# DeltaNet's convolution: the prompt's running sum moves into a PSUM bank, the key and recurrence chains get two banks instead of three, and sample rows get their own tanh

## The chip, the cores and the metric

The kernel runs on one core of a Trainium2 chip, in one launch. The metric is device time in microseconds. Names used below: TensorE (PE in the rows, PEld its weight loads) multiplies, VectorE (DVE), ScalarE (ACT) and GpSimd (POOL) work on tiles, SyncE (SP) issues DMAs. Each engine takes its instructions in the order in which they stand in its queue. PSUM is used here as eight banks of 128 x 512 fp32.

## The reference, cut to what matters

One step of a two-layer decoder: a gated DeltaNet layer with its feed-forward part, then a sparse-attention layer with its own. It is run for 512 prompt tokens and for 8 sample sequences of 4 tokens. The change touches the short convolution of the DeltaNet layer, and through the PSUM banks its key chain and recurrence:

```
def causal_short_conv(x, buf, w):
    xp = jnp.concatenate([buf.astype(x.dtype), x], axis=1)
    y = xp[:, 0:t] * w[0]
    for i in range(1, DN_CONV):              # DN_CONV = 4 taps
        y = y + xp[:, i:i + t] * w[i]
    return jax.nn.silu(y), xp[:, xp.shape[1] - (DN_CONV - 1):]
...
def step(S, xc):                             # recurrence over chunks
    U = wv_n - jnp.einsum('bhik,bhkv->bhiv', wk_n, S)
    O = jnp.einsum('bhik,bhkv->bhiv', qg_n, S) + jnp.einsum('bhij,bhjv->bhiv', aqk_n, U)
    S = gl_n[..., None, None] * S + jnp.einsum('bhik,bhiv->bhkv', kdec_n, U)
    return S, O
```

The convolved channels are q, k and v: 8 heads of 128 channels each, so 24 channel blocks. The silu is computed as a tanh and a product.

## The kernel before, in words

Channels lie on the 128 partitions, tokens along the free dimension: 512 prompt columns and 32 sample columns (8 x 4), 544 in all. A product with a weight is a `gemm` that takes both sides as a high and a low half and so issues three matmuls for each of 8 slices of the inner dimension (L177, L178, L179). A channel block is done in two halves of 256 and 288 columns, 24 matmuls each. `load_w` brings the weight in, casts the high half on ScalarE (L158) and subtracts for the low half on VectorE, or on GpSimd for q, v and z (L159).

`qkv(ty, h, ...)` makes one channel block; ty is 0 for q, 1 for k, 2 for v. ScalarE copies the gemm's banks into `pre` (L456, L458) and scales the first tap (L464). VectorE adds the other taps (L470); for q the second tap is made by ScalarE (L467) and added by GpSimd (L468). GpSimd makes the sample rows' sum with a product and an add for each tap (L475, L477). One tanh on ScalarE covers all 544 columns (L478); VectorE makes the prompt output (L479) and the sample output (L480).

`keys(h)`, K0 to K7 in the plan, turns a head's k block chunk by chunk: a transposition on TensorE (L525), a square with a sum on ScalarE (L526), products of k with itself (L533), which VectorE scales into BB (L535). After every fourth head DMAs put BB's diagonal blocks in DRAM. `diag_inverse(g)`, D0 and D1, takes four heads' blocks from there and solves them row by row on VectorE: a product L595 and a subtraction L597 for each step, 46 of each. ScalarE transposes the result (L600), DMAs carry it to DRAM and back, and `inverse(h)`, I0 to I7, builds the whole inverse of a chunk from it with small products (L621, L628, L629, L638, L641). `head(h)` is the recurrence over four chunks, whose products L722 to L729 depend on one another.

The plan of the DeltaNet part is a text: DN_START, then four pairs of heads whose recurrences are woven with other work, then a tail. In DN_START the letters k, q, v, z are channel blocks, the capitals what follows from them:

```
DN_START = "k0 K0 q1 k2 k1 K2 v1 k3 K1 z0 K3 S0 k4 q0 K4 Q0 v0 V1 D0 k5 q3 s0 v4 z1 Q1 V0 K5 s3 k6 k7 I0 q2 v3 I1 K6 Q3 K7 s2 Y0 Q2 s1 v2 V3"
```

The text sets the order in which the source is written. A scheduler then sorts each engine's queue by a simulated timeline, in which a tile has to be free before it is written; so the number of buffers of a tile decides what stands where. The banks are `mm` for gemms, `aux` for side products, and `ch` for the key chain and the recurrence.

Of the kernel before, what the change touches and what calls it, by code (L numbers as in the profile page):

```python
# [10 lines left out]
F32 = mybir.dt.float32  # L11
# [3 lines left out]
AF = mybir.ActivationFunctionType  # L15
OP = mybir.AluOpType
# [3 lines left out]
SEQ = 512  # L20
NB = 8
TS = 4
NS = NB * TS
NT = SEQ + NS
# [87 lines left out]
class Net:  # L112
# [206 lines left out]
    def deltanet(self, up, ctx):  # L319
        nc, A, O, T, V, S, G = self.nc, self.A, self.O, self.T, self.V, self.S, self.G  # L320
# [36 lines left out]
        wk = ctx.enter_context(tc.tile_pool(name="dnw", bufs=2))  # L357
# [16 lines left out]
        def decays():  # L374

            wab = self.load_w(W, 0, KD, 4 * D, 16)
            abf = wk.tile([128, NT], F32, name="cy")[0:16]
            for c0, cn in HALVES:
                ps = self.mm()[0:16, :cn]
                self.gemm(ps, wab, u, c0, cn)  # L380
# [26 lines left out]
            for n in (13, 11, 9, 7, 5, 3):  # L407
# [5 lines left out]
                                   op0=OP.mult, op1=OP.mult)  # L413
# [25 lines left out]
        def hb():  # L439

            return wk.tile([128, SEQ], F32, name="hb", tag="hb", bufs=HB)

        def qkv(ty, h, to, outS):

            o = to[h] = hb()
            ch = ty * 8 + h
            w = self.load_w(W, 0, KD, ch * 128, 128, pool_lo=ty != 1)
            pre = wk.tile([128, 515 + 56], F32, name="pre")
            pres = pre[:, 515:571].rearrange("p (b n) -> p b n", n=7)
            G.memset(pre[:, 0:3], 0.0)  # L450
            G.tensor_copy(pres[:, :, 0:3], hist[:, ch].rearrange("p (b n) -> p b n", n=3))
            for c0, cn in HALVES:
                ps = self.mm()[:, :cn]
                self.gemm(ps, w, u, c0, cn)
                n = min(cn, SEQ - c0)
                S.copy(pre[:, 3 + c0:3 + c0 + n], ps[:, 0:n])  # L456
                if n < cn:
                    S.copy(pres[:, :, 3:7], ps[:, n:cn].rearrange("p (b t) -> p b t", t=4))  # L458
                yield

            cw = [self.cw[:, i * 24 + ch:i * 24 + ch + 1] for i in range(4)]
            y = wk.tile([128, NT], F32, name="cy")
            th = wk.tile([128, NT], F32, name="cth", bufs=1)
            S.activation(y[:, 0:SEQ], pre[:, 0:SEQ], AF.Copy, scale=cw[0])  # L464
            if ty == 0:
                y2 = wk.tile([128, NT], F32, name="cth", bufs=1)[:, 0:SEQ]
                S.activation(y2, pre[:, 1:1 + SEQ], AF.Copy, scale=cw[1])  # L467
                G.tensor_tensor(y[:, 0:SEQ], y[:, 0:SEQ], y2, op=OP.add)  # L468
            for i in range(1 if ty else 2, 4):
                V.scalar_tensor_tensor(y[:, 0:SEQ], pre[:, i:i + SEQ], cw[i], y[:, 0:SEQ], op0=OP.mult, op1=OP.add)  # L470
            ys = y[:, SEQ:NT].rearrange("p (b t) -> p b t", t=4)
            ts = sm.tile([128, NB, TS], F32, name="cts")
            for i in range(4):
                wb = cw[i][:, :, None].to_broadcast([128, NB, TS])
                G.tensor_tensor(ts if i else ys, pres[:, :, i:i + 4], wb, op=OP.mult)  # L475
                if i:
                    G.tensor_tensor(ys, ys, ts, op=OP.add)  # L477
            S.activation(th, y, AF.Tanh)  # L478
            V.scalar_tensor_tensor(o, th[:, 0:SEQ], 1.0, y[:, 0:SEQ], op0=OP.add, op1=OP.mult)  # L479
            V.scalar_tensor_tensor(outS[:, h], th[:, SEQ:NT], 1.0, y[:, SEQ:NT], op0=OP.add, op1=OP.mult)  # L480

            g = h // 4
            left = rows.setdefault((ty, g), [sm.tile([128, 27, 4], F32, name=f"cl{ty}{g}", bufs=1), {*range(4 * g, 4 * g + 4)}])
            r = left[0]
            left[1].remove(h)
            S.copy(r[:, :, h % 4].rearrange("p (a b) -> p a b", b=3),
                   bass.AP(tensor=pre.tensor, offset=pre.offset + 512, ap=[list(pre.ap[0]), [7, 9], [1, 3]]))
            if not left[1]:
                pc = self.bank("ch")
                T.transpose(pc[0:108, 0:128], r.rearrange("p r h -> p (r h)"), ident)  # L490
                cso = wk.tile([108, 128], F32, name="cso", bufs=1)
                S.copy(cso, pc[0:108, 0:128])
                for dst, a, n in ((O["p_dn_conv"], 0, 3), (O["s_dn_conv"], 12, 24)):
                    self.dma(bass.AP(tensor=dst.tensor, offset=dst.offset + (8 * ty + 4 * g) * 128, ap=[[QKV, n], [128, 4], [1, 128]]),
                             cso[a:a + 4 * n])

        def kF(h):
            return qkv(1, h, kT, kS)
# [379 lines left out]
        def plan(text):  # L878
            return chain.from_iterable(make[t[0]](int(t[1])) for t in text.split())

        decays()
        run(plan(DN_START))
        for p, (text, inv, steps) in enumerate(DN_PAIRS):
# [860 lines left out]
    def run(self, ctx):  # L1744
# [4 lines left out]
        self.G.memset(self.nhalf, -0.5)  # L1749
        self.nvh = self.cst.tile([128, 1], F32, name="nvh")  # L1750
        self.cw = self.cst.tile([128, 96], F32, name="cw")
        self.banks(mm=3, aux=2, ch=3)
        with ExitStack() as c:
            og = self.deltanet(up, c)
        self.banks(mm=4, aux=4)
# [14 lines left out]
        with tc.tile_pool(name="nsa", bufs=1) as np_:  # L1770
# [6 lines left out]
            o = self.attention(ux, rstd, tiles, up, np_)  # L1777
# [39 lines left out]
```

## Time and profile before

| | |
|---|---|
| three runs, us | 1664.23, 1658.86, 1659.84; median 1659.84 |
| the profiled execution, us | 1663.51 |
| its span from first to last instruction, us | 1661.7 |
| mean granted TensorE clock | 0.985 |
| busy: TensorE, VectorE, ScalarE, GpSimd | 96%, 64%, 43%, 34% |
| DeltaNet part | from the start to about 400 us |

The rows below are of the profiled execution. A timeline row gives the start and the duration of an instruction (or of several of one form, x and their count), the engine, the source line, output and inputs; in brackets stands how long the engine was idle before it, and what ended that. Line numbers are those of the kernel before. Those of the changed kernel are one lower from L480 on (L525 is L524 there); within the convolution, scale, taps, tanh and output of the prompt are L466, L468, L469 and L470, the sample rows' products and adds L474 and L476, their tanh and output L478 and L479.

### The profile page before, as it was taken

How to read it: one execution, taken by the hardware profiler on the slowest of the kernel's cores; microseconds unless marked ns; L12 is line 12 of the kernel's file. 1: busy time of each engine (PE TensorE's matmuls, PEld its weight loads, DVE VectorE, ACT ScalarE, POOL GpSimd, SP SyncE). 2: the span in 40 equal slices, each digit the busy share in tenths (PEclk: the TensorE clock that was granted, in tenths of full speed). 3: DMA queues.
4: the chain of work that ended last, by engine and by line, in shares of the span. 5: the costliest groups of instructions: out<-in, count | busy, mean ns of one | idle time of the engine just before them, and what ended most of it. 6: DMA issues, size and time to landing. Idle time of an engine off the chain costs nothing.

```text
span 1661.7 us, 32748 instructions
## 1 busy us (share of the span) xinstructions
PE 1598.3 (96%) x12527; PEld 1528.5 (92%) x12527; DVE 1062.2 (64%) x2543; ACT 709.8 (43%) x1796; POOL 564.5 (34%) x861
## 2 busy tenths in 40 slices
PE   8998898998989999999999999999999999999997
PEld 7998788987989999999999999877999999999997
DVE  5879779487577753555556688678875553355533
ACT  5554554553323222232332487778843232132233
POOL 3675546424366711100145476565520000000000
PEclk9999999999999999999999999999999999999999
DMA  6233412257556634354342532523133332334222
GB/s 195 77 78 93 109 36 70 72 163 219 138 143 142 160 101 117 95 164 132 108 140 81 147 95 78 177 70 112 45 96 102 102 106 79 108 90 127 77 88 81
DMA packets 289069, 183.37 MB, mean 110 GB/s; under 512 B 25183, under 2 KB 271784, under 8 KB 288784
## 3 DMA queue, kind: packets, MB, share of 16 engines
q1 hardware_dynamic: 286352, 172.88, 37.5%
q0 software_dynamic: 2560, 8.39, 1.4%
q8 instruction: 99, 1.62, 0.4%
q14 instruction: 58, 0.48, 0.1%
HBM read 159.33 MB, written 26.90 MB: 112 GB/s over the span
## 4 chain that ended last, share of the span: by engine, by line
PE 77%; DVE 10%; POOL 4%; DMA 3%; ACT 3%; issue 2%; SPq 0%; POOLq 0%; DVEq 0%; ACTq 0%
PE mm L179 15%; PE mm L177 15%; PE mm L178 15%; PE aux L177 5%; PE aux L178 5%; PE aux L179 5%; PE po L1641 2%; PE aux L1668 2%; DVE hb L595 2%; DVE hb L597 1%; DVE wlo L159 1%; PE mm L1578 1%; PE mm L1579 1%; PE mm L818 1%; DVE cy L470 1%
## 5 line engine op out<-in xcount | busy, mean ns | idle before, releaser
L177 PE MATMUL mm<-uh,whi 128*128 128x288 f32 (+2 forms) x1824 | 531.3, 293 | 5.1 <-DVE hb L689 1.7
L179 PE MATMUL mm<-uh,wlo 128*128 128x288 f32 (+2 forms) x1824 | 523.8, 292 | 6.7 <-DVE wlo L159 6.7
L178 PE MATMUL mm<-ul,whi 128*128 128x288 f32 (+2 forms) x1824 | 530.1, 292 | 0.0
L158 ACT CAST whi<-wraw 128x1024 fp32r<-128x1024 f32 (+5 forms) x231 | 215.9, 936 | 524.0 <-PE mm L178 431.0
L177 PEld LDWEIGHTS mm<-uh,whi 128*128 128x128 f32 (+1 forms) x1824 | 343.9, 189 | 8.4 <-DVE hb L689 2.1
L179 PEld LDWEIGHTS mm<-uh,wlo 128*128 128x128 f32 (+1 forms) x1824 | 341.0, 189 | 9.2 <-DVE wlo L159 8.3
L178 PEld LDWEIGHTS mm<-ul,whi 128*128 128x128 f32 (+1 forms) x1824 | 344.3, 189 | 1.5 <-issue 0.4
L159 DVE TENSOR_TENSOR wlo<-wraw,whi 128x1024 fp32r<-128x1024 f32 (+5 forms) x207 | 235.5, 1138 | 118.6 <-ACT whi L158 117.2
L179 PE MATMUL aux<-uh,wlo 128*128 128x288 f32 (+1 forms) x704 | 202.7, 288 | 3.1 <-DVE wlo L159 3.1
L177 PE MATMUL aux<-uh,whi 128*128 128x288 f32 (+1 forms) x704 | 203.3, 289 | 0.0
L178 PE MATMUL aux<-ul,whi 128*128 128x288 f32 (+1 forms) x704 | 203.3, 289 | 0.0
L177 PE MATMUL mm<-hh,whi 128*128 128x256 f32 (+1 forms) x704 | 202.0, 289 | 0.0
L178 PE MATMUL mm<-hl,whi 128*128 128x256 f32 (+1 forms) x704 | 201.4, 288 | 0.0
L179 PE MATMUL mm<-hh,wlo 128*128 128x256 f32 (+1 forms) x704 | 196.5, 288 | 0.0
L179 PEld LDWEIGHTS aux<-uh,wlo 128*128 128x128 f32 x704 | 133.1, 189 | 3.6 <-DVE wlo L159 3.6
L184 POOL TENSOR_TENSOR ycol<-yvar,nhalf 128x2 f32<-128x2 f32 (+1 forms) x2 | 1.6, 775 | 390.2 <-DVE yvar L1716 390.2
L178 PEld LDWEIGHTS aux<-ul,whi 128*128 128x128 f32 x704 | 133.1, 189 | 0.0
L177 PEld LDWEIGHTS aux<-uh,whi 128*128 128x128 f32 x704 | 132.8, 189 | 0.2 <-issue 0.2
L178 PEld LDWEIGHTS mm<-hl,whi 128*128 128x128 f32 x704 | 132.6, 188 | 0.0
L177 PEld LDWEIGHTS mm<-hh,whi 128*128 128x128 f32 x704 | 132.6, 188 | 0.0
L179 PEld LDWEIGHTS mm<-hh,wlo 128*128 128x128 f32 x704 | 129.6, 188 | 0.0
L969 DVE SCALAR_TENSOR_TENSOR fup<-aux,rstd 128x256 f32<-128x256 f32 x88 | 38.6, 439 | 122.9 <-PE aux L179 122.9
(535 smaller groups left out, 2969.1 us busy)
## 6 DMA issues: line engine op xcount, KB each, us to landing
wraw<-in_ffn_w_in_dram SPq DMA_DIRECT2D x88, 512.0 KB
wraw<-in_dn_w_in_dram SPq DMA_DIRECT2D x32, 512.0 KB
wraw<-in_ffn_w_out_dram SPq DMA_DIRECT2D x32, 384.0 KB
wraw<-in_ffn_w_out_dram SPq DMA_DIRECT2D x32, 320.0 KB
hb<-in_state_dn_S_dram SPq DMA_DIRECT2D x32, 256.0 KB
wraw<-in_nsa_w_kv_dram SPq DMA_DIRECT2D x12, 512.0 KB
bskew<-bscr SPq DMA_DIRECT2D x16, 320.0 KB
x<-xd SPq DMA_DIRECT2D x16, 272.0 KB
```

Source lines behind the costliest of these rows:

```text
L158: self.S.copy(hi, src)
L159: (self.G if pool_lo else self.V).tensor_tensor(lo, src, hi.bitcast(F32), op=OP.subtract)
L177: self.T.matmul(ps, lhsT=hi[:, k, :], rhs=uh[:, cs], start=first and k == 0, stop=False)
L178: self.T.matmul(ps, lhsT=hi[:, k, :], rhs=ul[:, cs], start=False, stop=False)
L179: self.T.matmul(ps, lhsT=lo[:, k, :], rhs=uh[:, cs], start=False, stop=last and k == kc - 1)
L470: V.scalar_tensor_tensor(y[:, 0:SEQ], pre[:, i:i + SEQ], cw[i], y[:, 0:SEQ], op0=OP.mult, op1=OP.add)
L595: V.tensor_tensor(t, D[a][:, 0:m, l:l + 1].to_broadcast([64, m, n]), row.to_broadcast([64, m, n]), op=OP.mult)
L597: V.tensor_tensor(N[a][:, 0:m, l:32], N[a][:, 0:m, l:32], t, op=OP.subtract)
L818: T.matmul(ps, lhsT=Kh, rhs=um[q], start=True, stop=True)
L969: V.scalar_tensor_tensor(up, pu, 0.5, rstd[:, cs], op0=OP.mult, op1=OP.mult)
L1641: T.matmul(self.po, lhsT=self.VT[ty][:, kb, g], rhs=m[:, i:i + 2].rearrange("p e q -> p (e q)"), start=False, stop=last and kb > k0 and m ...
L1668: T.transpose(ps[:, i * 128:(i + 1) * 128], P[2 * pr + e][ty][:, a:a + 128], ident)
```

## The change

The running sum `y` of the prompt columns is no longer an SBUF tile with two buffers but a PSUM bank of its own with one buffer. The eight banks, split 3, 2 and 3 before, are split 3 (`mm`), 2 (`aux`), 2 (`ch`) and 1 (`cy`). For q too, all three later taps are made by VectorE. The sample rows keep an SBUF tile `ys`, and have their own tanh over 32 columns; the prompt's tanh over 512 columns and its output stand in the source ahead of the sample rows' sum.

```
-            abf = wk.tile([128, NT], F32, name="cy")[0:16]
+            abf = wk.tile([128, NT], F32, name="cth", bufs=1)[0:16]
...
-            y = wk.tile([128, NT], F32, name="cy")
+
+            y = self.bank("cy")
+            ys = wk.tile([128, NB, TS], F32, name="cy")
             th = wk.tile([128, NT], F32, name="cth", bufs=1)
-            S.activation(y[:, 0:SEQ], pre[:, 0:SEQ], AF.Copy, scale=cw[0])
-            if ty == 0:
-                y2 = wk.tile([128, NT], F32, name="cth", bufs=1)[:, 0:SEQ]
-                S.activation(y2, pre[:, 1:1 + SEQ], AF.Copy, scale=cw[1])
-                G.tensor_tensor(y[:, 0:SEQ], y[:, 0:SEQ], y2, op=OP.add)
-            for i in range(1 if ty else 2, 4):
-                V.scalar_tensor_tensor(y[:, 0:SEQ], pre[:, i:i + SEQ], cw[i], y[:, 0:SEQ], op0=OP.mult, op1=OP.add)
-            ys = y[:, SEQ:NT].rearrange("p (b t) -> p b t", t=4)
+            S.activation(y, pre[:, 0:SEQ], AF.Copy, scale=cw[0])
+            for i in range(1, 4):
+                V.scalar_tensor_tensor(y, pre[:, i:i + SEQ], cw[i], y, op0=OP.mult, op1=OP.add)
+            S.activation(th[:, 0:SEQ], y, AF.Tanh)
+            V.scalar_tensor_tensor(o, th[:, 0:SEQ], 1.0, y, op0=OP.add, op1=OP.mult)
             ts = sm.tile([128, NB, TS], F32, name="cts")
             for i in range(4):
                 wb = cw[i][:, :, None].to_broadcast([128, NB, TS])
                 G.tensor_tensor(ts if i else ys, pres[:, :, i:i + 4], wb, op=OP.mult)
                 if i:
                     G.tensor_tensor(ys, ys, ts, op=OP.add)
-            S.activation(th, y, AF.Tanh)
-            V.scalar_tensor_tensor(o, th[:, 0:SEQ], 1.0, y[:, 0:SEQ], op0=OP.add, op1=OP.mult)
-            V.scalar_tensor_tensor(outS[:, h], th[:, SEQ:NT], 1.0, y[:, SEQ:NT], op0=OP.add, op1=OP.mult)
+            ysf = ys.rearrange("p b t -> p (b t)")
+            S.activation(th[:, SEQ:NT], ysf, AF.Tanh)
+            V.scalar_tensor_tensor(outS[:, h], th[:, SEQ:NT], 1.0, ysf, op0=OP.add, op1=OP.mult)
...
-        self.banks(mm=3, aux=2, ch=3)
+        self.banks(mm=3, aux=2, ch=2, cy=1)
```

The scheduler's order moves with it. In the excerpts an x and a number after a shape count instructions, and the brackets name the engines and DMA queues whose semaphores an instruction waits for.

First, TensorE's queue at head 4's keys. Before, sample keys (L559, L562), the transpositions L525 and the products L533 stand among gemm matmuls:

```order
L559 MATMUL ch<-Bs,BsT 128x128 [waits DVE_49]
L525 MATMUL ch<-ct,hb 128x128 [waits Activation_49]
L705 MATMUL aux<-ct,hb 128x128 x2
L179 MATMUL mm<-uh,wlo 128x256
L533 MATMUL ch<-hb 128x128 [waits DVE_49,PE_49]
L533 MATMUL ch<-hb 128x128 x3
L177 MATMUL mm<-uh,whi 128x256
```

Of the change:

```order
L179 MATMUL mm<-uh,wlo 128x256
L524 MATMUL ch<-ct,hb 128x128 [waits DVE_49,PE_49]
L524 MATMUL ch<-ct,hb 128x128 [waits Activation_49]
L561 MATMUL ch<-B_1257,BsT 128x128 [waits DVE_49]
L524 MATMUL ch<-ct,hb 128x128 [waits Activation_49] x2
L532 MATMUL ch<-hb 128x128 [waits Activation_49]
L532 MATMUL ch<-hb 128x128 x3
L704 MATMUL aux<-ct,hb 128x128 [waits DVE_49]
L704 MATMUL aux<-ct,hb 128x128 x3
L515 MATMUL ch<-ct,Gc 128x128 [waits DVE_49]
L515 MATMUL ch<-ct,Gc 128x128 x3
L177 MATMUL mm<-uh,whi 128x288 [waits Activation_49]
```

The four transpositions of this head now follow one another with no gemm matmul between. The first of these products stood behind 588 gemm matmuls of DeltaNet and now stands behind 696; for head 3, whose products DMAs carry to D0, it is 475 and 539.

Second, ScalarE's queue where D0 ends (L600, and L599 in the change). Before:

```order
L458 COPY pre<-mm 128x8x4
L600 COPY hb<-hb 64x16x16 [waits DVE_49]
L600 COPY hb<-hb 64x16x16
L526 ACTIVATE junk_112,ssk<-ch 128x128 [waits PE_49]
L478 ACTIVATE cth<-cy 128x544 [waits DVE_49,Activation_49,Pool_49]
```

Of the change:

```order
L466 ACTIVATE cy<-pre,cw 128x512 [waits DVE_49,Pool_49]
L478 ACTIVATE cth<-cy 128x32 [waits Activation_49,Pool_49]
L485 COPY cl_1013<-pre 128x27 [waits Activation_49]
L525 ACTIVATE junk_112,ssk<-ch 128x128 [waits PE_49]
L469 ACTIVATE cth<-cy 128x512 [waits DVE_49]
L525 ACTIVATE junk_112,ssk<-ch 128x128 [waits PE_49]
L158 CAST whi<-wraw 128x1024 [waits DMAHW2_49,PE_49]
L646 ACTIVATE cth<-hb 128x512 [waits DVE_49]
L466 ACTIVATE cy<-pre,cw 128x512
L599 COPY hb<-hb 64x16x16 [waits DVE_49]
L599 COPY hb<-hb 64x16x16
```

The scale L466 of a block waits for VectorE, which has to be done with the block ahead in the one bank. The tanh of the sample rows stands ahead of that of the prompt. D0's copies come behind a cast that comes behind the start part's last gemms.

Third, TensorE's queue at the first inverse, I0. Before, its first products L621 stand among gemm matmuls, behind 978 of the 1008 that the start part has:

```order
L179 MATMUL mm<-uh,wlo 128x256
L621 MATMUL aux<-XT,BB 128x96 [waits DMAHW5_49,DMAHW4_49,DMAHW3_49]
L621 MATMUL aux<-XT,BB 128x96 x3
L177 MATMUL mm<-uh,whi 128x256
```

Of the change:

```order
L524 MATMUL ch<-ct,hb 128x128 [waits Activation_49]
L673 MATMUL ch<-ct,q2s 128x1 [waits Activation_49,Pool_49]
L620 MATMUL aux<-XT,BB 128x96 [waits DMAHW7_49,DMAHW6_49,DMAHW0_49]
L620 MATMUL aux<-XT,BB 128x96 x3
L675 MATMUL ch<-qS,kS 128x128 [waits DVE_49]
...
L637 MATMUL aux<-XT,BB 64x64 [waits DVE_49]
L637 MATMUL aux<-XT,BB 64x64 x3
L620 MATMUL aux<-XT,BB 128x96 [waits DVE_49,PE_49,Activation_49]
L620 MATMUL aux<-XT,BB 128x96 x3
L640 MATMUL aux<-XX,Y_120 64x64 [waits DMAHW5_49,DMAHW1_49,DVE_49]
```

All 1008 gemm matmuls of the start part now stand ahead of the first inverse, and none between the first (I0) and the second (I1), whose first products are the second L620.

## Rows read from the trace of the kernel before

**Rows 1.** The page's busy times (us, share of the span, instructions) and its chain by engine.

```profile
PE 1598.3 (96%) x12527; PEld 1528.5 (92%) x12527; DVE 1062.2 (64%) x2543; ACT 709.8 (43%) x1796; POOL 564.5 (34%) x861
...
PE 77%; DVE 10%; POOL 4%; DMA 3%; ACT 3%; issue 2%; SPq 0%; POOLq 0%; DVEq 0%; ACTq 0%
```

**Rows 2.** Busy time by stretch: length, each engine (instructions), clock, DMA share, GB/s.

```profile
118.50:179.20 60.70, 51.22 (x400) 48.45 (x399) 55.61 (x147) 27.31 (x71) 37.28 (x60) 0.94 0.30 80
179.20:200.00 20.80, 18.75 (x158) 17.96 (x158) 13.64 (x34) 13.08 (x42) 13.09 (x26) 0.92 0.63 147
200.00:212.00 12.00, 11.97 (x104) 9.16 (x105) 8.47 (x31) 6.89 (x22) 1.34 (x6) 1.00 0.38 84
```

**Rows 3.** TensorE's waits from 40 to 200: us in total, times, longest.

```profile
PE ch L525 <- ACT junk L526: 9.5, 3, 4.6
```

**Rows 4.** Timeline from 133 to 143: start, duration, engine, line, idle time before it.

```profile
135.56 4.17 POOL L477 TENSOR_TENSOR cy<-cy,cts 128x32 f32<-128x32 f32 x1
...
137.56 0.28 PE L179 MATMUL mm<-uh,wlo 128*128 128x256 f32 x1
...
140.78 0.25 POOL L477 TENSOR_TENSOR cy<-cy,cts 128x32 f32<-128x32 f32 x1
...
141.06 0.66 ACT L478 ACTIVATE cth<-cy 128x544 f32<-128x544 f32 x1 [6.38 <-POOL cy L477]
...
141.75 0.69 DVE L479 SCALAR_TENSOR_TENSOR hb<-cth,cy 128x512 f32<-128x512 f32 x1 [2.14 <-ACT cth L478]
...
142.44 0.48 PE L525 MATMUL ch<-ct,hb 128*128 128x128 f32 x1 [4.61 <-ACT junk L526]
```

**Rows 5.** Convolution lines, whole span: min/median/max ns and starts, or busy, mean | idle.

```profile
L470 DVE SCALAR_TENSOR_TENSOR cy<-pre,cw,cy x64: 645/750/2806, 40.5 to 302.6; 128x512 f32<-128x512 f32 x64
...
L468 POOL TENSOR_TENSOR cy<-cy,cth 128x512 f32<-128x512 f32 x8 | 10.4, 1303 | 6.8 <-ACT cth L467 6.8
...
L467 ACT ACTIVATE cth<-pre,cw 128x512 f32<-128x512 f32 x8 | 5.7, 714 | 4.5 <-DVE hb L479 2.9 <-DVE qS L480 0.9 <-DVE zs L691 0.7
...
L477 POOL TENSOR_TENSOR cy<-cy,cts 128x32 f32<-128x32 f32 x72 | 34.1, 474 | 4.9
...
L478 ACT ACTIVATE cth<-cy x24: 641/659/669, 43.8 to 303.5; 128x544 f32<-128x544 f32 x24
...
L480 DVE SCALAR_TENSOR_TENSOR kS<-cth,cy x8: 177/185/2367, 45.1 to 169.5; 128x32 f32<-128x32 f32 x8
```

**Rows 6.** Two VectorE lines that read one operand from PSUM: min/median/max ns, starts.

```profile
L755 DVE SCALAR_TENSOR_TENSOR BB<-aux,nvh,hb x8: 734/748/752, 276.3 to 402.4; 128x512 f32<-128x512 f32 x8
...
L689 DVE SCALAR_TENSOR_TENSOR hb<-cth,mm x16: 405/411/422, 83.5 to 365.6; 128x256 f32<-128x256 f32 x16
```

**Rows 7.** D0's first loop line, then the timeline from its end to the next gemm.

```profile
L595 DVE TENSOR_TENSOR hb<-hb x46: 159/269/2431, 118.5 to 178.2; 64x48 f32<-64x48 f32 x3, 64x60 f32<-64x60 f32 x3, 64x15 f32<-64x15 f32 x2, 64x28 f32<-64x28 f32 x2
...
179.13 1.17 ACT L600 COPY hb<-hb 64x256 f32<-64x256 f32 x2 [5.74 <-DVE hb L597]
...
187.47 1.03 PE L621 MATMUL aux<-XT,BB 128*128 128x96 f32 x8
...
194.91 0.29 PE L179 MATMUL mm<-uh,wlo 128*128 128x288 f32 x1
...
195.97 1.13 PE L621 MATMUL aux<-XT,BB 128*128 128x96 f32 x8
...
200.45 0.68 PE L638 MATMUL aux<-XT,BB 128*64 128x64 f32 x8
...
212.20 0.36 PE L177 MATMUL mm<-uh,whi 128*128 128x256 f32 x1
```

**Rows 8.** Timeline of the last pair of heads, TensorE, from 375 to 387.

```profile
375.80 0.39 PE L725 MATMUL ch<-hb,XX 128*128 128x128 f32 x2
...
378.41 0.39 PE L725 MATMUL ch<-hb,XX 128*128 128x128 f32 x2
...
386.89 0.47 PE L801 MATMUL mm<-ct,B 128*128 128x128 f32 x1 [2.54 <-DVE B L799]
```

## The prediction

> **What bounds the kernel now.** The page comes first. TensorE is busy for 96% of the span and carries 77% of the chain that ended last; VectorE carries 10% of it [rows 1]. So the time is TensorE's work plus the moments in which it stands still, and a change to the convolution, which takes no matmul away, can only move those moments. The convolution's 24 tanhs run from 43.8 to 303.5 us [rows 5]. Behind the DeltaNet part, which ends near 400 us, the changed program has the same instructions in the same order as before, so those last 1260 us cannot differ except by where they start.
>
> Second, the waits of TensorE from 40 to 200 us. One line dominates: the transposition L525 of a key chunk waits for ScalarE's sum of squares L526, three times, 9.5 us in all [rows 3]. Third, the timeline around the longest one. Gemm matmuls end at 137.56. GpSimd's add L477 for the sample rows, 0.25 us as a rule, started at 135.56 and took 4.17 us. ScalarE's tanh L478, which covers prompt and sample rows, waits 6.38 us for the next of these adds, L526 stands behind the tanh in ScalarE's queue, and L525 starts at 142.44 [rows 4]. What the reader is to see is a chain through three queues: a slow GpSimd add, a tanh behind it, a copy behind the tanh, TensorE behind that.
>
> Fourth, diag_inverse(0), D0 below: a VectorE loop (L595, L597), 46 of each, from 118.5 to 179.1, where ScalarE's L600 follows it [rows 7]. In these 60.7 us VectorE is busy 55.6 [rows 2]: in this stretch it is the limit, not TensorE (51.2). L600 had waited 5.74 us for D0's last step, with further squares L526 queued behind it. After D0, DMAs carry the result round, the first inverse product L621 starts at 187.47, the start part's last gemm matmul at 194.91, and gemm work is back at 212.20 [rows 7]. From 200 to 212 TensorE is busy all the time, but on small dependent products [rows 2].
>
> **The change, part by part.**
>
> *Taps.* A tap L470 takes 0.750 us at the median with both streams in SBUF [rows 5]. No row shows VectorE writing PSUM. The nearest ones read it: 0.748 for 128x512, 0.411 for 128x256 [rows 6]. Bounds for a tap: 0.69, the output L479 of the same size [rows 4], and 0.82, twice L689's; over 72 taps that is -4 to +5 us on VectorE. I take 0.75, no change, since L755 has the same size and a PSUM input. The eight q blocks get a tap more, 8 x 0.75 = 6.0 us on VectorE, and lose 5.7 us on ScalarE (L467) and 10.4 us on GpSimd (L468) [rows 5]. These two engines have idle time, VectorE in D0 has almost none.
>
> *Contention.* GpSimd's add takes 0.25 us when alone and took 4.17 [rows 4]; its mean of 0.474 over 72 makes 72 x 0.224 = 16 us of excess [rows 5]. A VectorE sample output has a median of 0.185 us and took 2.367 in one case, which lies in D0 [rows 5]. So two-stream VectorE work and GpSimd work do hold each other up. With the sum in PSUM a tap has one SBUF stream left, and rows with one (L755 734 to 752 ns, L689 405 to 422) never get long [rows 6]. In D0 this saves VectorE that one case, 2.367 - 0.185 = 2.2 us, and the bounds are 0 (L595 and L597 still have two SBUF streams and meet the same GpSimd work) and 9 (three more such cases among the loop's own steps, which reach 2.431 us at a median of 0.269 [rows 7]). The Trainium skill, SBUF — State Buffer, section "Who interferes with whom", says that a VectorE instruction with two SBUF inputs contends with a GpSimd instruction that reads SBUF, and one with at most one does not. Here the trace agrees (4.17 against 0.25 us). By that rule alone the wait of 9.5 us would go, and the time would be that of rival 1.
>
> *Own tanh for sample rows.* This adds 24 small tanhs and splits the chain of rows 4. But in the changed order the sample tanh L478 still stands ahead of the prompt tanh L469 in most blocks (the ScalarE excerpt shows one), so ScalarE still waits for GpSimd there. I cost it at nothing: 24 x about 0.2 us (VectorE's output of the same 32 columns is 0.185 [rows 5]) on ScalarE, which has idle time; if that cover is gone, 4.8 us.
>
> *Two banks for keys and recurrence, one for the sum.* This is the part that moves instructions. K3's last products, whose results D0 needs, stood behind 475 gemm matmuls and now stand behind 539: 64 more at 51.2 / 400 = 0.128 us [rows 2] is 8 us. K4's keys, laced between gemms before, stand together in the first TensorE excerpt, where each L524 waits for the ScalarE square ahead of it and nothing else is between: I allow 5.5 us, from 0 (hidden) to 7 (a 4.6 us wait as in rows 3 and half of another). D0's start thus moves from 118.5 to about 132 (126.5 to 134).
>
> D0's own length: 60.6 us, plus 5 taps and 2 outputs more between its first and last row (18 and 7 by the order, 13 and 5 before), 5 x 0.75 + 2 x 0.69 = 5.1, minus the 2.2 above, minus the 5.1 in which VectorE is now idle [rows 2] and which the queue of more work fills: 58. Bounds 53 and 63. D0 ends at 190 (before 179.1).
>
> From D0's end to the return of gemm work was 33.1 us (212.20 - 179.1 [rows 7]) with gemm work in between. Now no gemm is left at that point: the second TensorE excerpt shows the first inverse product behind the last gemm and both inverses without any between. Worked out from rows 7: copies and DMAs 8.3 (179.13 to 187.47), first inverse until the second may start 4.5 (195.97 to 200.45 of the second), then 16.2 (195.97 to 212.20): 29.0. The lower bound is 8.3 + 4.5 + 12.0 = 24.8, with only the bare stretch of rows 2 at the end. I take 27. Gemm work returns at 190 + 27 = 217 against 212.2: +5 (from 126.5 + 53 + 24.8 = 204, -8, to 134 + 63 + 29 = 226, +14).
>
> *Later.* Pairs 0 to 2 have gemm work to fill with: 0, give or take 3. In the last pair the chain of chunks with two banks starts wholly behind the last gemm, about 1.5 chunks more at 2.6 us (375.80 to 378.41); but the sample products from L801 on, at 386.89, end the part, 8 us and more behind these chunks [rows 8], so most of it is hidden: +1 (0 to 4).
>
> Sum: +5 + 1 = +6 on the profiled execution's 1663.5, 1669.5. That execution lies 3.7 us over the median of the runs (1659.84), so the median should go to **1666**.
>
> **Rivals.**
>
> 1. *Relief: faster.* The stalls of rows 3 go (9.5 us), and D0 is not the limit. For it: every long GpSimd add in rows 4 and 5. Against it: D0's start in the order. It decides if D0 starts by 127 and takes at most 52 us, with 25 us behind it: gemm work is back by 204, -8, and with the whole 9.5 the time is 1650 to 1652.
>
> 2. *Nothing to measure.* The relief on GpSimd pays for the later keys: 9.5 us won, 8 to 10 lost, VectorE 6.0 up for the taps and about 6 down in contention. For it: the sample tanh still waits for GpSimd. About 1660.
>
> 3. *Queueing on one bank: slower by more.* The scale L466 of the next block waits for the output L470 of this one, and in ScalarE's queue the square L525 and the copies out of the gemm banks stand behind it. A block holds the bank for at least 0.72 + 3 x 0.75 + 0.66 + 0.69 = 4.3 us (tanh and scale L467 from rows 5), several times that while D0's steps lie between. The profile has 24 blocks in 260 us [rows 5], 11 us apart, which speaks against it. Two or three stalls of 4.6 us [rows 3] on top of the forecast make 1675 to 1680; it decides when a hold passes 11 us outside D0. The Trainium skill, Perfetto Trace Analysis, section "Optimization Strategy", says that a bubble that repeats on the engine that should be busy can mean too little PSUM for the next tile. By it, with one bank less for the keys, the stalls at L525 would grow in number; no row of before shows two banks.
>
> **How the numbers follow.** 0.3% of 1660 is 5 us, and that is about what a measurement of this kernel can tell from no change. Forecast: chance 0.50, own range 1660 to 1677; a quarter of it falls within 0.3%. Relief 0.26, nearly all faster. Nothing to measure 0.14. Queueing 0.10. So faster 0.26, same 0.26, slower 0.48. The range goes from 1650, which cuts off part of the relief case, to 1679, which cuts off the end of the queueing case.
>
> **What would show it.** Right: VectorE's first L594 near 132 and last near 190, no gemm matmul between the first L620 and some 27 us behind D0's end, gemm back near 217, a bare patch of L524 with waits near 127 to 133. Long GpSimd adds gone outside D0's steps; taps near 0.75. Wrong: D0 starting before 127, or ending before 184 (relief); many waits of L466 for L470 with L524 behind (queueing); taps above 0.8 us; the common part taking a different time from its start to its end.

## The result and the profile after

The changed kernel takes 1676.45 us (median of four runs, 1674.02 to 1678.93), the kernel before 1659.35 (1656.90 to 1664.23): a ratio of 1.0099, 95% interval 1.0070 to 1.0129. It is slower by 17 us; forecast were 6, with a range to 1679.

The page's busy times and chain of the changed kernel answer to [rows 1]:

```profile
PE 1606.6 (96%) x12527; PEld 1531.0 (91%) x12527; DVE 1052.7 (63%) x2551; ACT 709.9 (42%) x1812; POOL 526.9 (31%) x853
...
PE 79%; DVE 10%; DMA 3%; issue 2%; ACT 2%; POOL 2%; SPq 1%; POOLq 0%; DVEq 0%; ACTq 0%
```

VectorE and GpSimd have less to do than before (9.5 and 37.6 us), and the kernel is slower all the same. The convolution's lines, over the whole span (min/median/max ns, first and last start):

```profile
L468 DVE SCALAR_TENSOR_TENSOR cy<-pre,cw,cy x72: 667/748/758, 44.4 to 317.0; 128x512 f32<-128x512 f32 x72
...
L470 DVE SCALAR_TENSOR_TENSOR hb<-cth,cy x24: 671/683/690, 48.2 to 318.4; 128x512 f32<-128x512 f32 x24
...
L476 POOL TENSOR_TENSOR cy<-cy,cts x72: 245/253/472, 44.7 to 314.9; 128x32 f32<-128x32 f32 x72
```

A tap into PSUM takes 0.748 us, as one into SBUF did, and none is long any more: 758 ns at most where it was 2806 [rows 5]. GpSimd's add is at most 472 ns where one of 4.17 us held ScalarE [rows 4]. ScalarE's waits from 30 to 420 us (total, times, longest) say the same; the 28.9 us in which the tanh waited for GpSimd (first line, of before) have become 2.3:

```profile
ACT cth L478 <- POOL cy L477: 28.9, 10, 6.4
```

```profile
ACT cth L469 <- DVE cy L468: 20.8, 13, 4.4
...
ACT cth L478 <- POOL cy L476: 2.3, 3, 1.0
```

So what the change promises at its own place has come: from 40 us to the end of the start part's last gemm matmul TensorE is busy 143.8 us before and after, and stands still for 5.2 us in place of 11.5. The time goes elsewhere. D0 starts 20 us later, and this is the chain to its first step in the changed kernel, from the timelines of TensorE, VectorE, SyncE and VectorE again:

```profile
118.59 0.27 PE L524 MATMUL ch<-ct,hb 128*128 128x128 f32 x1
...
119.30 0.17 DVE L506 TENSOR_SCALAR sB<-ssk 128x4 f32<-128x4 f32 x1 [2.78 <-ACT junk L525]
...
119.98 1.12 DVE L534 SCALAR_TENSOR_TENSOR BB<-ch,sB,hb 128x128 f32<-128x128 f32 x4
...
121.14 2.80 SPq L155 DMA_DIRECT2D scr<-BB  x4
125.23 6.83 SPq L155 DMA_DIRECT2D wraw<-in_dn_w_in_dram  x2
132.23 1.15 SPq L155 DMA_DIRECT2D hb<-scr  x2
...
136.43 1.13 DVE L534 SCALAR_TENSOR_TENSOR BB<-ch,sB,hb 128x128 f32<-128x128 f32 x4
...
138.31 0.25 DVE L594 TENSOR_TENSOR hb<-hb 64x16 f32<-64x16 f32 x1 [0.16 <-POOL hb L587]
```

and the same chain before:

```profile
100.81 0.27 PE L525 MATMUL ch<-ct,hb 128*128 128x128 f32 x1
...
103.66 1.12 DVE L535 SCALAR_TENSOR_TENSOR BB<-ch,sB,hb 128x128 f32<-128x128 f32 x4
...
104.80 1.98 SPq L155 DMA_DIRECT2D scr<-BB  x4
108.31 0.39 SPq L155 DMA_DIRECT2D wraw<-in_dn_w_in_dram  x1
108.88 1.15 SPq L155 DMA_DIRECT2D hb<-scr  x2
```

The reader is to see two steps. Head 3's last transposition for the square starts at 118.59 in place of 100.81, and without its sum the scaling cannot run. Then D0's loads (hb<-scr) stand behind two weight loads in SyncE's queue, the second of which goes out 6 us late, and leave at 132.23, 11 us behind the stores; before it was 4. Head 4's scaling (136.43) stands ahead of D0's first step in VectorE's queue too. But the first step counts for nearly all: before, D0's first step came 9.6 us behind its loads, now 6.1, so that from the transposition to D0 it is 17.7 us before and 19.7 now. Of the 19.8 us by which D0 is late, 17.8 lie ahead of the square and 2.0 behind it.

Not all of the 17.8 comes from the change. Run 11 below has the same instructions in the same order on TensorE up to 131 us, and its transposition starts at 115.79, 2.8 us sooner. The two traces part ahead of 40 us, 1.2 us in the first 20 (mean granted clock 0.83, and 1.00 in run 11) and 1.6 from 36.6 to 40, where the granted clock was at its lower level (0.50, 1.2 GHz) in the profile of the change and at its upper one in that of run 11. Busy time by stretch of the change, then of run 11 with its transposition:

```profile
36.60:40.00 3.40, 3.40 (x15) 3.36 (x16) 0.00 (x0) 0.65 (x3) 2.09 (x1) 0.50 0.11 15
```

```profile
36.60:40.00 3.40, 3.40 (x28) 3.20 (x27) 0.79 (x4) 0.94 (x2) 0.82 (x1) 1.00 0.32 72
...
115.79 0.27 PE L524 MATMUL ch<-ct,hb 128*128 128x128 f32 x1
```

D0 itself takes 58.8 us (138.3 to 197.1), before 60.6. Five of its steps take over 0.8 us, as before (11.3 us together, before 9.6). Its last step shows that contention is not gone where both VectorE operands still lie in SBUF: it took 2.21 us beside a GpSimd subtraction of 2.35. From VectorE's and GpSimd's timelines:

```profile
194.67 2.35 POOL L159 TENSOR_TENSOR wlo<-wraw,whi 128x1024 fp32r<-128x1024 f32 x1
...
194.85 2.21 DVE L596 TENSOR_TENSOR hb<-hb 64x31 f32<-64x31 f32 x1
```

The stretch behind it, in busy time by stretch (D0, D0's end to the first inverse product, from there to the next gemm; columns as in [rows 2]):

```profile
138.30:197.10 58.80, 51.46 (x394) 47.36 (x393) 56.75 (x151) 28.73 (x81) 31.06 (x64) 0.96 0.26 68
197.10:204.40 7.30, 3.89 (x15) 2.88 (x15) 5.23 (x18) 3.79 (x14) 0.89 (x3) 0.50 0.50 120
204.40:228.70 24.30, 22.91 (x172) 18.94 (x172) 10.19 (x35) 9.28 (x29) 1.34 (x6) 0.73 0.37 86
```

and on TensorE's and ScalarE's timelines, which answer to [rows 7]:

```profile
188.76 0.29 PE L179 MATMUL mm<-uh,wlo 128*128 128x288 f32 x1
192.86 1.44 PE L532 MATMUL ch<-hb 128*128 128x128 f32 x8 [3.81 <-ACT junk L525]
...
197.10 1.17 ACT L599 COPY hb<-hb 64x256 f32<-64x256 f32 x2 [2.24 <-DVE hb L596]
...
197.95 0.44 PE L524 MATMUL ch<-ct,hb 128*128 128x128 f32 x1 [2.52 <-DVE GL L518]
...
204.37 2.02 PE L620 MATMUL aux<-XT,BB 128*128 128x96 f32 x8 [0.73 <-DMA XT<-scn]
...
228.68 0.36 PE L177 MATMUL mm<-uh,whi 128*128 128x256 f32 x1
```

The start part's gemms are done at 189, six us sooner than before: that is the smaller idle time from above. But then it has nothing to fill the time until D0's result is back, the granted clock is 0.50 (1.2 GHz) from 197 to 204 and 0.73 in the mean of the next 24 us, and gemm work returns at 228.7 in place of 212.2. That difference of 16.5 is nearly the whole loss; 2.8 of it is the early low clock. Before, the start part's gemms were still there to fill the same stretch until 195.2 [rows 7].

The last pair of heads adds a little: from the last gemm ahead of it to the first behind the DeltaNet part it is 29.2 us (386.2 to 415.4), before 25.3 (371.1 to 396.4).

Behind that, the two programs are the same, and yet this part, from its first gemm matmul to the start of TensorE's last instruction, took 1254.9 us in the profile of before and 1250.5 in that of the change; over all profiles of this study it lies between 1241 and 1257. The granted clock stood at its lower level for 17 us of it before, for 7 in the change and not at all in run 2, which has the 1241; that this is the whole reason is not shown. So the experiments below are read at the start of the first gemm matmul behind the DeltaNet part, which the edits can move, and by the ratios of many runs.

### The profile page after: what moved, and what is told of

Read it like the earlier page. It is cut to its first block, busy times and chain, and to the rows that moved or that the text cites. A ratio compares the mean times of both kernels' runs of the same rounds, so it can differ in the third digit from the quotient of the medians.

```text
span 1676.4 us, 32763 instructions
## 1 busy us (share of the span) xinstructions
PE 1606.6 (96%) x12527; PEld 1531.0 (91%) x12527; DVE 1052.7 (63%) x2551; ACT 709.9 (42%) x1812; POOL 526.9 (31%) x853
## 4 chain that ended last, share of the span: by engine, by line
PE 79%; DVE 10%; DMA 3%; issue 2%; ACT 2%; POOL 2%; SPq 1%; POOLq 0%; DVEq 0%; ACTq 0%
PE mm L177 16%; PE mm L179 16%; PE mm L178 16%; PE aux L179 5%; PE aux L177 5%; PE aux L178 5%; PE po L1640 3%; PE aux L1667 2%; DVE wlo L159 2%; DVE hb L596 1%; SPq L155 1%; PE mm L1577 1%; DVE hb L594 1%; PE mm L1578 1%; DVE cy L468 1%
## 5 line engine op out<-in xcount | busy, mean ns | idle before, releaser
L177 PE MATMUL mm<-uh,whi 128*128 128x288 f32 (+2 forms) x1824 | 531.3, 293 | 8.3 <-ACT pre L456 2.1
L177 PEld LDWEIGHTS mm<-uh,whi 128*128 128x128 f32 (+1 forms) x1824 | 342.9, 188 | 14.0 <-ACT pre L456 3.0
L177 PE MATMUL aux<-uh,whi 128*128 128x288 f32 (+1 forms) x704 | 202.8, 288 | 0.0
L177 PE MATMUL mm<-hh,whi 128*128 128x256 f32 (+1 forms) x704 | 202.0, 289 | 0.0
L177 PEld LDWEIGHTS mm<-hh,whi 128*128 128x128 f32 x704 | 132.6, 188 | 0.0
L177 PEld LDWEIGHTS aux<-uh,whi 128*128 128x128 f32 x704 | 132.3, 188 | 0.2 <-issue 0.2
```

Source lines behind the costliest of these rows:

```text
L177: self.T.matmul(ps, lhsT=hi[:, k, :], rhs=uh[:, cs], start=first and k == 0, stop=False)
```

## The experiments

Three theories. 1: the lost bank of keys and recurrence places the keys, and with them D0, later in every queue, so that the gemms run out ahead of D0's end. 2: the single bank of the sum makes scale, tanh and squares queue on ScalarE. 3: the eight more taps on VectorE lengthen D0. The readings of all runs (D0's first step and the first copy behind its last; "gemm back", the first gemm matmul behind the 1008 of the start part; the first gemm matmul behind the DeltaNet part; us). The times are of one profile each, and the granted clock ahead of 40 us, lowest in the change and in run 5, moves them by up to 3 us:

| run | D0 | gemm back | behind DeltaNet | ratio to before (95%) |
|---|---|---|---|---|
| before | 118.5 to 179.1 | 212.2 | 396.4 | |
| the change | 138.3 to 197.1 | 228.7 | 415.4 | 1.0099 (1.0070 to 1.0129) |
| 1 two banks alone | 134.8 to 193.4 | 226.2 | 416.6 | 1.0090 (1.0055 to 1.0125) |
| 2 sum in SBUF, three banks | 122.3 to 183.2 | 214.2 | 400.8 | 1.0003 (0.9983 to 1.0022) |
| 3 PSUM sum, bank from the gemms | 113.1 to 171.9 | 212.5 | 390.3 | 0.9965 (0.9944 to 0.9986) |
| 4 keys and D0 first | 108.2 to 165.7 | 219.1 | 413.9 | 1.0100 (1.0066 to 1.0134) |
| 5 key products elsewhere | 127.7 to 186.7 | 219.7 | 405.1 | 1.0035 (1.0015 to 1.0055) |
| 6 SBUF sum, two gemm banks | 120.4 to 169.4 | 223.5 | 407.3 | 1.0062 (1.0039 to 1.0084) |
| 7 matmuls behind D0 | 136.8 to 195.0 | 237.0 | 428.0 | 1.0164 (1.0141 to 1.0187) |
| 8 sum in aux | 122.2 to 177.8 | 215.2 | 409.7 | 1.0067 (1.0046 to 1.0088) |
| 9 D0's DMAs on ScalarE | 137.9 to 197.1 | 228.6 | 417.2 | 1.0120 (1.0092 to 1.0147) |
| 10 run 3 with them | 117.4 to 172.8 | 215.1 | 393.9 | 0.9975 (0.9956 to 0.9995) |
| 11 D0 ahead of K4 | 127.8 to 187.4 | 217.7 | 405.1 | 1.0041 (1.0022 to 1.0060) |
| 12 run 3 with that | 107.5 to 168.9 | 215.8 | 392.2 | 0.9986 (0.9970 to 1.0003) |

**1. Two banks alone.**

```
-        self.banks(mm=3, aux=2, ch=3)
+        self.banks(mm=3, aux=2, ch=2)
```

> The kernel before with two banks instead of three for keys and recurrence, and nothing else changed (one bank stays unused). Theory 1 (the order): the lost bank alone moves the squares of head 3 behind more gemm matmuls (598 instead of 524 in the queue, 602 in the changed kernel), D0 starts later, its end falls behind the last gemm of the start part, and the inverses run bare, in part at half clock. It expects most of the loss: +10 to +18 us, D0's first step at 130 or later, gemm work back near 225. Theory 2 (one bank for the sum makes scale, tanh and squares queue): no such bank here, so within 4 us of the kernel before. Theory 3 (8 more taps on VectorE lengthen D0): no such taps here, within 4 us.

The kernel before with one bank less has the loss of the change: 1.0090. Its VectorE line of D0, and the gemm that comes back:

```profile
L595 DVE TENSOR_TENSOR hb<-hb x46: 165/275/2491, 134.8 to 191.7; 64x48 f32<-64x48 f32 x3, 64x60 f32<-64x60 f32 x3, 64x15 f32<-64x15 f32 x2, 64x28 f32<-64x28 f32 x2
...
226.24 0.36 PE L177 MATMUL mm<-uh,whi 128*128 128x256 f32 x1
```

No sum in PSUM, no tap more, no tanh more: theories 2 and 3 cannot explain this. Theory 1 stands, with all three of its marks.

**2. The changed convolution in SBUF, with three banks.**

```
-            y = self.bank("cy")
-            ys = wk.tile([128, NB, TS], F32, name="cy")
+            yt = wk.tile([128, NT], F32, name="cy")
+            y = yt[:, 0:SEQ]
+            ys = yt[:, SEQ:NT].rearrange("p (b t) -> p b t", t=4)
...
-        self.banks(mm=3, aux=2, ch=2, cy=1)
+        self.banks(mm=3, aux=2, ch=3)
```

> The changed convolution (three VectorE taps for q too, own tanh for the sample rows) with its sum in SBUF as before, and three banks for keys and recurrence. Theory 1: head 3's last square stands behind 531 gemm matmuls, near the 524 of before, so D0 starts within 3 us of 118.5; -3 to +6 us in all, as the first inverse product stands behind 1004 of 1008. Long GpSimd adds (over 2 us) are back. Theory 2: within 4 us of before. Theory 3: the taps make the loss, +8 to +17 us.

1.0003, with long GpSimd adds (up to 2633 ns); D0 starts at 122.3, a little outside the 3 us. The extra taps and the tanh of its own neither cost nor bring what a measurement can tell; this is what theory 1 gives, and it settles theory 3.

**3. The bank taken from the gemms.**

```
-        self.banks(mm=3, aux=2, ch=2, cy=1)
+        self.banks(mm=2, aux=2, ch=3, cy=1)
```

> The changed kernel with the bank for the sum taken from the gemms (two banks) in place of the key chain (three banks). Theory 1: head 3's last square stands behind 490 gemm matmuls and the first inverse product behind 978, so the loss is gone and the relief on GpSimd counts: -10 to +3 us against before, unless two gemm banks cost waits of TensorE for ScalarE's copies, which then show as L177 waiting for L456. Theory 2: the single bank for the sum still queues, +8 to +17 us. Theory 3: +8 to +17 us.

0.9965, faster than before, and faster than the change by its whole loss and more. The one bank of the sum is still there, so theory 2 falls here a second time as the cause of this loss. D0 starts at 113.1.

**4. The keys and D0 first in the text.** DN_START begins "k0 K0 k2 K2 k1 K1 k3 K3 D0 q1 v1 z0 S0 q0 Q0 v0 V1 k4 K4 k5"; the banks are those of the change.

> The changed kernel with another text for the start part: the k blocks, their keys and D0 first, the same items behind them. Theory 1: D0 starts near 100 to 108, the first inverse product stands behind 832 of 1008 gemm matmuls, so gemms fill the chain behind D0 and the clock stays up: faster than the changed kernel by 15 to 30 us, 1645 to 1662. Theory 2: one bank for the sum queues as before, so within 5 us of the changed kernel's 1676. Theory 3: VectorE's work is the same and D0 as long, gain at most 6 us.

A miss for theory 1. D0 starts at 108.2 as forecast, and the first inverse product has gemms to follow, but the ratio is 1.0100, the number that theory 2 forecast. TensorE stands still ahead of D0: from 85 to 117 us it is busy 18.8 us, in the change 30.1. Its waits from 40 to 215 us, the longest of them, and what stands ahead of it on VectorE and ScalarE:

```profile
PE mm L177 <- ACT pre L456: 7.9, 2, 7.5
PE ch L524 <- ACT junk L525: 3.1, 5, 1.1
```

```profile
108.20 0.17 DVE L594 TENSOR_TENSOR hb<-hb 64x16 f32<-64x16 f32 x1 [1.74 <-DMA hb<-scr]
108.30 0.67 DVE L470 SCALAR_TENSOR_TENSOR hb<-cth,cy 128x512 f32<-128x512 f32 x1
...
109.01 0.69 ACT L466 ACTIVATE cy<-pre,cw 128x512 f32<-128x512 f32 x1 [8.45 <-DVE hb L470]
...
113.17 0.61 PE L177 MATMUL mm<-uh,whi 128*128 128x288 f32 x1 [7.50 <-ACT pre L456]
```

D0's first step waits for its load, and the output L470 of a block stands behind it in VectorE's queue. Until that output is made, the one bank of the sum is not free: ScalarE waits 8.45 us before the scale L466 of the next block, and the copy L456, which frees a gemm bank, stands behind it. So the longest stall of this run is the queueing of theory 2 and rival 3; with this order it costs, where in the change the same wait is 2.5 us at most. What is won behind D0 (9.6 us at the next gemm) is given back by the first gemm behind the DeltaNet part but for 1.5. So an early D0 alone does not bring the time back; how much of this run's loss is the key chain's missing bank is not shown.

**5. The key products' tile from the side products' banks.** In `keys`, the third tile:

```
             betas(hcols(h))
-            ps = self.bank("ch")
+            ps = self.aux()
```

> The changed kernel, with the key products' tile (the third that a head's keys take) from the side products' banks in place of the two key and recurrence banks. Theory 1a (the keys lack the bank, so D0 starts late): head 3's last square stands behind 525 gemm matmuls again (524 before, 602 changed), D0 starts near 120, time 1655 to 1666, that is 10 to 20 us under the changed kernel. Theory 1b (the recurrence lacks the bank, which still has two): at most 5 us under the changed kernel, D1 and the last pair as late as there.

1.0035, two thirds of the loss gone: 11 us under the change by the ratios, as forecast for the case 1a, though its median (1667.24, with 1662.78 for before beside it) lies just above the 1655 to 1666 named there. Head 3's last square is back at 105.56, but D0 starts at 127.7 and not near 120: 22 us lie between the two, and gemm work is back 7.5 us later than before. What remains is also in part the recurrence, which still has two banks: from the last gemm ahead of the last pair to the first behind it, 29.2 us (375.9 to 405.1), the same as in the change, where three banks take 25.3.

**6. The partner of run 3: the convolution of before, two gemm banks.**

```
-        self.banks(mm=3, aux=2, ch=3)
+        self.banks(mm=2, aux=2, ch=3)
```

> The kernel before with two gemm banks instead of three and nothing else (one bank unused): the partner of the run with the sum in PSUM and two gemm banks, which came out at 0.9965. If the PSUM sum's relief on GpSimd made that gain, this one is slower than it by 5 to 10 us, 1654 to 1665, with GpSimd adds over 2 us. If the order that two gemm banks bring made it, this one is as fast, 1645 to 1653.

1.0062 where run 3 has 0.9965, a wider gap than the 5 to 10 us forecast. So two gemm banks are no gain by themselves, and the changed convolution is worth some 16 us there. GpSimd's add of run 3, then of this run:

```profile
L476 POOL TENSOR_TENSOR cy<-cy,cts x72: 248/253/443, 40.4 to 292.1; 128x32 f32<-128x32 f32 x72
```

```profile
L477 POOL TENSOR_TENSOR cy<-cy,cts x72: 244/253/1582, 41.2 to 308.7; 128x32 f32<-128x32 f32 x72
```

The tanh's wait for GpSimd is 11.0 us there and 38.3 here. The two runs differ in the order as well, so how much of the 16 us is this wait is not shown.

**7. TensorE kept busy behind D0.** In `inverse(0)` of the changed kernel, ahead of its first product:

```
+            if h == 0:
+                warm = self.aux()
+                for i in range(10):
+                    T.matmul(warm, lhsT=solved[0][:, 0:128], rhs=solved[0], start=True, stop=True)
```

> The changed kernel with 10 matmuls of 128x512 more on D0's result, thrown away, ahead of the first inverse product, to keep TensorE busy while the DMAs run. If the low clock from 193 to 217 is a good part of the loss, the clock is back at full by 206, the stretch from D0's end to the next gemm falls from 33.6 to 26 to 30 us, and the time is 3 to 7 us under the changed kernel, 1669 to 1674. If the chain waits for VectorE, ScalarE and DMAs, it stays within 2 us of 33.6 or grows by the up to 6 us of the added matmuls.

The ratio is 1.0164. The added matmuls took 17.4 us, not 6, and the clock did not come back under them; from D0's end to the next gemm it is 42.0 us in place of 31.6 (33.6 as the expectation counts it), longer than either case had it. TensorE's timeline, then busy time by stretch:

```profile
195.67 17.43 PE L622 MATMUL aux<-hb 64*128 64x512 f32 x20 [1.99 <-ACT hb L599]
...
215.00 1.86 PE L625 MATMUL aux<-XT,BB 128*128 128x96 f32 x8
...
237.01 0.36 PE L177 MATMUL mm<-uh,whi 128*128 128x256 f32 x1
```

```profile
200.00:204.00 4.00, 4.00 (x6) 1.67 (x5) 0.00 (x0) 0.40 (x1) 0.00 (x0) 0.50 0.37 61
...
212.00:216.00 4.00, 4.00 (x16) 2.98 (x15) 0.00 (x0) 0.37 (x2) 0.00 (x0) 0.50 0.23 66
216.00:220.00 4.00, 2.85 (x26) 2.13 (x24) 0.99 (x4) 1.69 (x8) 0.00 (x0) 0.87 0.00 0
220.00:224.00 4.00, 3.61 (x39) 3.15 (x40) 3.21 (x13) 0.99 (x4) 0.00 (x0) 1.00 0.15 22
```

It still answers the question. From the first inverse product to the next gemm, this run has its clock back early and needs 22.0 us (215.0 to 237.0); the change, at half clock for over half of it (mean 0.73), needs 24.3, and run 11, at 0.93, needs 23.7. The low clock there is worth up to some 2 us of the loss; the rest of this stretch stays when the clock is up.

**8. The sum in a side product bank, three banks for keys.**

```
-            y = self.bank("cy")
+            y = self.aux()
...
-        self.banks(mm=3, aux=2, ch=2, cy=1)
+        self.banks(mm=3, aux=2, ch=3)
```

> The changed convolution with the sum in one of the two side product banks, three banks for keys and recurrence, three for gemms. Theory 1a: head 3's last square stands behind 532 gemm matmuls and the first inverse product behind 984 of 1008, D0 starts near 120: 1648 to 1660. Theory 2 (a bank held long by the sum blocks those that share it): side products wait, TensorE waits of aux grow over 5 us, 1662 to 1675.

1.0067, in theory 2's range, though TensorE's wait for a side product bank is not what grew; the longest sum is 9.8 us of L177 waiting for ScalarE's copies L456. D0 is early (122.2) and gemm work is back at 215.2, 3.0 us behind the kernel before; at the end of the part it is 13.3 behind. The 10 us arise between 280 and 330 us, in the pairs of heads; what holds them is left open, and theory 1, which forecast 1648 to 1660, does not cover this run.

**9 and 10. D0's DMAs issued by ScalarE,** in the change and in run 3: the stores in `keys` and the loads in `diag_inverse` by `self.nc.scalar.dma_start` in place of `self.dma`.

> The changed kernel with the eight key block stores and the four loads of D0 and D1 issued by ScalarE in place of SyncE. In the changed kernel D0's loads stood in SyncE's queue behind two weight loads and were issued at 132.2, 11 us behind the stores, and D0's first step stood in VectorE's queue behind head 4's key scaling; here that step stands ahead of it. If these two places are the 6 us that D0 started later than forecast, D0 starts at 126 to 132 in place of 138.3 and the time is 3 to 8 us under the changed kernel's (ratio to before 1.005 to 1.008). If only the missing bank counts, D0 starts at 136 or later and the ratio stays at 1.009 to 1.011. Against: ScalarE's own work waits behind the DMA issues.

> The run with the sum in PSUM, two gemm banks and three for keys and recurrence (ratio 0.9965), with the DMAs around D0 and D1 issued by ScalarE as in the run beside it. There D0 started at 113.1, about as soon as its data were there, and SyncE's queue was not named; so the two should be the same within 0.3%, 0.993 to 0.999 of before. If the queue of SyncE holds D0 and D1 there too, 0.991 or less; if ScalarE's issues cost more than they bring, 1.000 or more.

Run 9 gives no answer on SyncE. Its stores left at 118.56, but the loads stand behind head 4's squares in ScalarE's queue and leave at 135.12, later than before the edit; D0 starts at 137.9 and the ratio is 1.0120. Run 10 is the same as run 3 within their intervals, as expected.

**11 and 12. One item of the text moved,** in the change and in run 3:

```
-K3 S0 k4 q0 K4 Q0 v0 V1 D0 k5
+K3 S0 k4 q0 D0 K4 Q0 v0 V1 k5
```

> The changed kernel with one item of the start text moved: D0 ahead of K4 in place of behind V1. TensorE's queue keeps head 3's last square behind 602 gemm matmuls and the first inverse product behind all 1008, but D0's first step stands ahead of head 4's key scaling in VectorE's queue, and D0's loads one weight load behind the stores in SyncE's. Theory 1 with its late D0 as the price: D0 starts at 124 to 130 in place of 138.3, ends at 181 to 189, gemm work is back 6 to 14 us earlier than 228.7, ratio to before 1.002 to 1.007. If D0's place is not what counts (what it delays on VectorE and TensorE costs as much as it brings), D0 starts early but gemm work is back within 4 us of 228.7 and the ratio stays at 1.008 to 1.012.

> The run with the sum in PSUM, two gemm banks and three for keys and recurrence (ratio 0.9965), with the same item moved: D0 ahead of K4. The first inverse product stands behind 934 gemm matmuls in place of 978. If an earlier D0 pays wherever TensorE runs bare behind it, gemm work is back 3 to 8 us earlier than 212.5 and the ratio is 0.991 to 0.995. If D0 there already starts as soon as its data come (113.1), nothing changes: 0.994 to 0.999. Slower than before (1.002 and over) if it delays head 4's keys.

Run 11: head 3's last square and the first inverse product stand behind as many gemm matmuls as in the change, but D0's loads leave at 122.73 in place of 132.23. On SyncE's timeline:

```profile
118.34 2.84 SPq L155 DMA_DIRECT2D scr<-BB  x4
...
122.73 1.16 SPq L155 DMA_DIRECT2D hb<-scr  x2
```

D0 starts 10.5 us sooner, gemm work is back 11.0 sooner, the DeltaNet part ends 10.3 sooner, and the ratio is 1.0041. But 2.8 us of each are the early low clock, which this profile has not: the square, ahead of everything that the edit moves, is 2.8 us sooner already. From the square to D0 it is 12.0 us in place of 19.7. So D0's place is worth 7.7 us of D0's start, 8.2 at the next gemm and 7.5 at the end of the part: it is passed on in full, and the ratios, which rest on 11 and 4 executions, agree (1.0099 to 1.0041, 9.6 us). Run 12 brings nothing on top of run 3 (0.9986, its interval reaches 1.0003): D0 starts 5.6 us earlier there and ends 3.0 earlier, but gemm work is not back sooner. Run 3 stays the best version found, 0.9965 of the kernel before.

## Why the prediction came out as it did

**The direction and the mechanism were right.** The bank taken from the keys decides (run 1), by way of a later D0, no gemm left behind it, and a bare chain of inverses; run 11 shows the way over D0 for 7.5 us of the loss, the rest of it is read from the traces. The range held the time. The size was too small: 6 us forecast, 17 measured.

**Taps at no cost: right.** 0.748 us into PSUM. **Contention: right as far as it went.** The long adds are gone from the trace. The rule of the Trainium skill, SBUF — State Buffer, section "Who interferes with whom", agrees with that (472 ns at most, before 4166). What would have followed by that rule alone, rival 1, did not come: TensorE stands still 6 us less ahead of D0's end, but D0's end set the time. Run 3, where D0 is not late, gains 6.1 us on the kernel before; at the next gemm it is still 0.3 us behind, so the gain comes later, and that it is this relief and not the order is not shown.

**Own tanh: right.** Run 2, with it and the extra taps, is 1.0003.

**D0's start, "from 118.5 to about 132 (126.5 to 134)": the step that failed.** It came at 138.3, outside its bounds. I took head 3's products as the gate, 64 gemm matmuls later and 8 us, and added 5.5 us for head 4's keys. The gate is head 3's last square, since the scaling needs its sum: 78 gemm matmuls later in the listing (602 for 524), and 17.8 us later in the trace (118.59 for 100.81). Of these 17.8, 4.4 are there at the same count already (the 524th gemm matmul starts at 105.12 for 100.68, 2.8 of it the early low clock), and the 78 with what stands among them take 13.4. From the square to D0 it is 2.0 us more than before. I did not follow this path, with the DMAs' place in SyncE's queue and D0's first step behind head 4's scaling in VectorE's; with D0 in another place it takes 7.7 us less (run 11). By an estimate from these rows, without the 2.8 us D0 would start at 135.5, still outside the bounds.

**D0's length, 58: right in size,** 58.8, **in part by luck.** VectorE's busy time in it rose by 1.1 us and not by the 2.9 of the sum, though the long steps did not get fewer; its idle time fell by 3.0 and not by 5.1. The two misses nearly cancel. **D0's end to the next gemm, 27 (24.8 to 29.0): too short,** 31.6 (197.1 to 228.7). Its three pieces measured 7.3, 6.8 and 17.5 us where the upper bound had 8.3, 4.5 and 16.2: the first inverse until the second starts (204.37 to 211.18) was too short above all. The bound's inverses came from a stretch at full clock; the half clock is up to some 2 us of the difference (run 7). The last heads' key steps, which run at the same time and wait for VectorE and ScalarE (the row at 197.95), I had left out.

**The last pair, +1 (0 to 4): too small within its bound,** 3.9, and 3.9 too with only the key products moved away (run 5).

**Sum.** Start +19.8, length -1.8, behind it -1.5: 16.5 at the next gemm in place of 5. **The common part:** I said that it cannot differ except by its start, and named a different time as a sign of being wrong. It does differ, by 4.4 us between the two profiles and by 16 over all of them, so a single profile's span does not tell the loss.

**Rival 3** did not decide here: ScalarE waits 8.5 us in six pieces for the sum's bank, and TensorE's gemms wait for ScalarE's copies 3.8 us in all up to 440 us. In the order of run 4 it did cost, 7.5 us in one piece. The rule of the Trainium skill, Perfetto Trace Analysis, section "Optimization Strategy", on bubbles and too little PSUM would have had the stalls at the squares grow in number. From 40 to 200 us TensorE waits for a square six times in the change (6.3 us) and five in run 1 (6.7), three times before (9.5): more often, as that rule has it, but for less time. The missing bank's price showed in the order, not in these gaps.

## What to carry to other kernels

Where a scheduler orders the queues, a bank taken from a chain is paid at the chain's consumers: follow the order of what they need last (here a sum of squares, two queues and a DMA issue further on) and not only of the products that they read. A kernel may gain all that a change promises at its own place and lose it at a stage that nobody edited; look for the stretch in which the bounding engine runs out of filler, and ask who is late there. Before two profiles are subtracted, compare them at a point ahead of the edit: here 2.8 us of the difference stood there already. And try every donor before giving up a tile's new place: the same PSUM sum was 1% slower with a bank from the keys, 0.7% slower in a bank shared with the side products, and 0.35% faster with one from the gemms.

## What had not been expected of the hardware

Ten source matmuls of 64 x 512 fp32 ran as twenty instructions of 0.87 us at half clock; TensorE was busy from 195.7 to 213.0 without a gap, and the granted clock stayed at 0.50 to 216, then rose to 0.87 and 1.00 under small inverse products with pauses between (run 7).
